# Inverting the 64x64 triangles of two head pairs side by side, every second period

## The chip, the cores and the metric

The kernel runs on one core of one Trainium2 chip. The metric is the device time of one execution in microseconds (us). The core has five engines with a queue each: TensorE (PE, matmuls; PEld are its weight loads), VectorE (DVE), ScalarE (ACT), GpSimd (POOL) and SyncE (SP), which here issues the DMAs.

## The reference

Two layers over 256 tokens of width 2048. Layer 0 is RWKV-7 time mixing and an MLP, layer 1 chunked attention and an MLP; every sub-layer is normalised and modulated by shift, scale and gate vectors that are products of a vector `c` with a large matrix `w_ada`. The change lies in the time mixing, whose core is a recurrence for each of 32 heads of 64:

```python
def step(S, inp):
    r_t, w_t, k_t, v_t, kk_t, a_t = inp
    sa = jnp.einsum('bhvk,bhk->bhv', S, -kk_t)
    S = (S * w_t[:, :, None, :] + sa[..., None] * (kk_t * a_t)[:, :, None, :]
         + v_t[..., None] * k_t[:, :, None, :])
    y = jnp.einsum('bhvk,bhk->bhv', S, r_t)
    return S, y
mod = c @ w_ada[layer] + b_ada[layer]
```

## The kernel before

The recurrence is done in four chunks of 64 tokens. Within a chunk it is a triangular system, and the kernel inverts its 64x64 unit triangle for every head and chunk. Two heads make a pair (128 partitions); there are 16 pairs. A pair goes through four stages:

- `proj_steps` (dense work): the k and r projections, 16 weight blocks each, every block a 128x512 and a 128x256 matmul (L401, L402). Weights come as raw float32 tiles of 512 KB (`raw`), are rounded to a high half `wH` on ACT (L367), and DVE makes the low half `wL` (L370).
- `early`: decay, keys and norms, mostly on DVE and ACT.
- `invert`: the Gram matrices (L100, tile `gr`), then five levels of doubling. A level has two calls of `tiles`, each 16 matmuls of 32x32 on four 32x32 blocks of the array (L106, tile `iv`; the last level 8): first `al` (masked by POOL, L233) times `tt` (DVE's transpose of `u`, L229), copied by ACT to `xs` (L235), then `xs` times `u`, added to `u` by DVE (L246). `uf` holds the finished inverse.
- `late`: the chain over the four chunks, 16 short steps of PE, ACT and DVE (tiles `chn`, `py`, `zs`).

The loop of `layer_a` over `p` runs periods; in each one four neighbouring pairs are in the four stages, so there are 16 + 3 periods. A period has 16 slots. In a slot the small stages (`late`, `invert`, `early`) each take their share of steps and the dense stage takes its own; `tc.issue_after` makes them alternate on PE. In the last three periods no projection is left, and `out_steps` (part of the output projection `w_o`, 44 steps of six matmuls) is the dense work; `DRAIN_STEPS` says how many of its steps each of them gets. In six slots of every period (`ADA_SLOTS`) one tile of the modulation is done: a DMA of 512 KB into `raw` and one multiply-add of 128x1024 on DVE (L443, tile `acc`). Weights and modulation tiles share one ring of `RAW_BUFS` = 6 raw buffers, and all their DMAs go in order through the SP queue, as do the small tables `lw` (L121) and `lg` (L123).

Engines run their queues in order. [...]

Of the kernel before, what the change touches and what calls it, by code (L numbers as in the profile page):

```python
# [12 lines left out]
F32 = mybir.dt.float32  # L13
F32R = mybir.dt.float32r
AF = mybir.ActivationFunctionType
ALU = mybir.AluOpType
# [60 lines left out]
class Pair:  # L77
# [24 lines left out]
    def tiles(self, o, lhsT, rhs, pairs):  # L102

        for c in range(4):
            for R, K in pairs:
                self.b.nc.tensor.matmul(o[QS[K], c, :], lhsT[QS[R], c, :], rhs[QS[R], c, :], start=True, stop=True,  # L106
                                        tile_position=(H * R, H * K))

# [8 lines left out]
    def early(self):  # L117
        b, nc, j, k, r, v, s, ch = self.b, self.b.nc, self.j, self.k, self.r, self.v, self.s, self.ch
        pw, vec, cst, e01 = b.pw, b.vec, b.cst, self.e01
        lw = pw.tile([96, 2, P], F32, tag="lw", bufs=2, name="lw")  # L120
        nc.sync.dma_start(out=lw, in_=b.d["lora2"][j, :96, 0:2])  # L121
        self.lg = pw.tile([P, 2, P], F32, tag="lg", bufs=2, name="lg")
        nc.sync.dma_start(out=self.lg, in_=b.d["lora2"][j, :, 2:4])  # L123
# [24 lines left out]
        self.pc = pw.tile([P, 4, 1], F32, tag="pc", bufs=3, name="pc")  # L148
# [9 lines left out]
        self.bh, self.kh = s("bh", 2), s("kh", 2)  # L158
# [8 lines left out]
        kr = self.kr = self.big("kr", 3)  # L167
# [9 lines left out]
        bk = self.bk = pw.tile([P, 3, 4, C], F32, tag="bk", bufs=3, name="bk")  # L177
# [9 lines left out]
    def invert(self):  # L187
        b, nc, s, ch, kr, bk, bh, kh = self.b, self.b.nc, self.s, self.ch, self.kr, self.bk, self.bh, self.kh
        cst, pp = b.cst, b.pp

        def every(name):
            return cst(name).unsqueeze(1).to_broadcast([P, 4, H])

        def half(name, bufs):
            return b.pw.tile([P, 4, H], F32, tag=name, bufs=bufs, name=name)


        ui = cst("ui").unsqueeze(1).to_broadcast([P, 4, P])
        ts = []
        for src in (bh, kh):  # L200
            t = s()
            nc.gpsimd.tensor_tensor(out=ch(t), in0=ch(src), in1=self.pc.to_broadcast([P, 4, C]), op=ALU.mult)
            ts.append(t)
        pg = pp.tile([P, 4, P], F32, tag="gr", bufs=1, name="gr")
        self.each(lambda c: pg[:, c, :], lambda c: ch(bh)[:, c, :], lambda c: kr[:, c, :])
        ar = self.ar = s("ar", 2)
        nc.vector.tensor_tensor(out=ch(ar), in0=pg[:, :, C:P], in1=ui[:, :, C:P], op=ALU.mult)


        da, co, u = half("da", 2), half("co", 2), half("u", 2)  # L210
        for i, K in enumerate(QS):
            n = H * (i % 2)
            nc.scalar.copy(da[K], pg[K, :, n:n + H])
            if i % 2 == 0:
                nc.scalar.mul(co[K], pg[K, :, H:C], -1.0)
        nc.gpsimd.tensor_tensor(out=u, in0=da, in1=every("lev0"), op=ALU.mult)
        yield
        nc.vector.tensor_tensor(out=u, in0=u, in1=every("eye_h"), op=ALU.add)

        pt = b.psm().rearrange("p (a c k) -> p a c k", a=2, c=4)  # L220
        for i, t in enumerate(ts):
            self.each(lambda c: pt[:, i, c, :], lambda c: ch(t)[:, c, :], lambda c: cst("eye"))
        nc.scalar.copy(bk[:, 0:2], pt)
        yield
        uf = self.u = b.uf[self.j % 2]
        down, up = ((0, 1), (2, 3)), ((1, 0), (3, 2))
        for l in range(1, 6):
            tt_, xs = half("tt", 1), half("xs", 1)
            nc.vector.transpose(out=tt_.rearrange("p c t -> p (c t)"), in_=u.rearrange("p c t -> p (c t)"))  # L229
# [12 lines left out]
            yield
            pi = pp.tile([P, 16, H], F32, tag="iv", bufs=1, name="iv")[:, 0:4, :]
            if l < 5:
                self.tiles(pi, xs, u, [(i, i) for i in range(4)])
                nc.vector.tensor_tensor(out=u, in0=u, in1=pi, op=ALU.add)  # L246
            else:
                self.tiles(pi, xs, u, up)
                for K in QS[::2]:
                    nc.vector.tensor_copy(uf[K, :, H:C], pi[K])  # L250
            if l == 2:
                pg = pp.tile([P, 4, P], F32, tag="gr", bufs=1, name="gr")
                self.each(lambda c: pg[:, c, :], lambda c: ch(kh)[:, c, :], lambda c: kr[:, c, :])
                mk = self.mk = self.big("mk", 2)
                nc.vector.tensor_tensor(out=mk, in0=pg, in1=ui, op=ALU.mult)
            yield

    def late(self):
# [7 lines left out]
        for c in range(4):  # L266
            pch = pp.tile([P, 3, C], F32, tag="chn", bufs=1, name="chn")
# [38 lines left out]
        rg = s("sl", 3)  # L306
# [4 lines left out]
        for i in range(2):  # L311
            nc.tensor.matmul(pg, self.lg[:, i, :], self.tg[:, i, :], start=(i == 0), stop=(i == 1))
# [5 lines left out]
class Body:  # L318
    RAW_BUFS = 6
    W_BUFS = 3  # L320
    DRAIN_STEPS = (14, 14, 16)
    ADA_SLOTS = (1, 3, 6, 9, 11, 14)

# [15 lines left out]

    @contextmanager  # L340
# [8 lines left out]
    def raw(self, src, shape=None, ada=False):  # L349
# [3 lines left out]
        else:  # L353
            t = self.wp.tile([P, HK * P], F32, tag="raw", bufs=self.RAW_BUFS, name="raw")
# [18 lines left out]
    def weight_part(self, src, lo, hi):  # L373

        half, at = lo // HK * HK * P, lo % HK * P
        t = self.wp.tile([P, HK * P], F32, tag="raw", bufs=self.RAW_BUFS, name="raw")
# [185 lines left out]
    def run(self):  # L562
# [16 lines left out]
        self.lazy, self.fins, self.ada_pool = False, iter(()), None  # L579
        self.ada_done = set()  # L580
# [4 lines left out]
        with ExitStack() as st:  # L585
# [7 lines left out]
            nxt = self.out_proj(self.pp, "w_o", self.y_hl, (0, 2), "g_mlp0", (0, 4), (0, 3), self.o_ps)  # L593
            sp.close()
            with ExitStack() as s2:
                pp = s2.enter_context(tc.tile_pool(name="ps_m0", bufs=2, space=bass.MemoryType.PSUM, reuse_waits="tile"))
                self.psm = lambda: pp.tile([P, 512], F32, tag="m", bufs=2, name="m")
                s2.enter_context(self.ada_room(5))
                nxt = self.mlp(s2, pp, 0, *nxt, "g_kv", ("kv", 1), ("kv", 0))
            with ExitStack() as s2:  # L600
                pp = s2.enter_context(tc.tile_pool(name="ps_at", bufs=2, space=bass.MemoryType.PSUM, reuse_waits="tile"))
                self.psm = lambda: pp.tile([P, 512], F32, tag="m", bufs=1, name="m")
                s2.enter_context(self.ada_room(3))
# [15 lines left out]
    def layer_a(self, st, sp):  # L619
# [6 lines left out]
        with ExitStack() as s1:  # L626
# [5 lines left out]
            pb = self.np = s3.enter_context(tc.tile_pool(name="pb", bufs=1))  # L632
            h = ph.tile([P, KT, T + 1], F32, name="h")
# [154 lines left out]
            for i in range(4):  # L788
                v_part(3, i, "tm"[i % 2])
            s3.close()  # L790
# [13 lines left out]
        with ExitStack() as s1:  # L804
# [5 lines left out]
            self.uf = [pw.tile([P, 4, C], F32, name=f"uf_{i}") for i in range(2)]  # L810
# [6 lines left out]
            def proj_steps(pr):  # L817
                for dst, hl in (("k", xk), ("r", xr)):
# [14 lines left out]
            def out_steps():  # L833
# [3 lines left out]
                sums, todo = self.o_ps, [(n, 0, HK) for n in range(4)] + [(n, HK, KT - 2) for n in range(4)]  # L837
                for n, lo, hi in todo + [(n, 0, HK) for n in range(4, 8)]:
# [349 lines left out]
```

## Time and profile before

| | |
|---|---|
| time, median of 3 runs | 2720.82 us (2719.59 to 2724.55) |
| profiled execution: time, span | 2718.15 us, 2716.3 us |
| PE, DVE, ACT, POOL busy | 97%, 77%, 50%, 9% of the span |
| granted TensorE clock, mean | 0.993 |
| time mixing with its periods | from 210 us to 753 us of the span |

In the tables of windows each engine has its busy time and the number of instructions in the window, then come the granted TensorE clock, the busy share of the DMA engines and their rate. A row of the timeline has the start, the time it is in flight, and xN for N instructions merged; one small float32 matmul is two records there. Matmuls overlap, so what a group costs PE is read from its start to the start of the next group.

### The profile page before, as it was taken

To read this page: it belongs to the slowest core of one execution; us is meant where nothing else is said; L and a number is where in the kernel's file an instruction comes from. 1 tells how busy PE (TensorE), PEld (TensorE's weight loads), DVE (VectorE), ACT (ScalarE), POOL (GpSimd) and SP (SyncE) were. 2 spreads that over 40 slices of the span, in tenths; PEclk is the share of its full clock that TensorE was granted. 3 is DMA by queue.
4 is the path that set the end of the run, shared out by engine and by line. 5 is a ranking of instruction groups with operands and counts; after the bars stand their busy time and mean duration, and the time that the engine had idled before them with its cause. 6 is when DMAs were issued, how large, how long until landed. Compare 5 with 4: busy or idle time off the path is not lost.

```text
span 2716.3 us, 58473 instructions
## 1 busy us (share of the span) xinstructions
PE 2646.6 (97%) x23690; PEld 2237.0 (82%) x23690; DVE 2098.3 (77%) x3109; ACT 1347.4 (50%) x2432; POOL 235.0 (9%) x368
## 2 busy tenths in 40 slices
PE   6998999999999999999999999999999999999997
PEld 3777777777889888888888898877898888888886
DVE  5779887778788798888988898899987556555555
ACT  3344554455455536445355554465565364453553
POOL 0002232232210000000000100000100000000002
PEclk8999999999999999999999999999999999999999
DMA  9967665555587799888988768887857555555553
GB/s 334 314 232 254 201 194 172 161 175 172 190 279 256 251 342 332 309 310 317 331 318 319 249 225 309 310 292 252 285 194 258 186 189 189 187 186 187 187 188 122
DMA packets 217390, 662.64 MB, mean 244 GB/s; under 512 B 21408, under 2 KB 68896, under 8 KB 217120
## 3 DMA queue, kind: packets, MB, share of 16 engines
q1 hardware_dynamic: 215056, 656.36, 71.3%
q8 instruction: 186, 3.05, 0.4%
q10 hardware_dynamic: 2064, 2.54, 0.3%
q14 instruction: 84, 0.69, 0.1%
HBM read 656.72 MB, written 2.10 MB: 243 GB/s over the span
## 4 chain that ended last, share of the span: by engine, by line
PE 86%; DVE 4%; DMA 2%; issue 2%; ACT 1%; POOL 0%; DVEq 0%; SPq 0%; ACTq 0%; POOLq 0%
PE pj L401 45%; PE pj L402 22%; PE iv L106 2%; PE pj L391 2%; PE pj L392 2%; PE pj L390 2%; PE gr L100 1%; DVE wL L370 1%; DVE acc L443 1%; PE ms L100 1%; PE o L390 1%; PE ms L110 1%; PE chn L270 1%; DMA rada<-w_ada 1%; PE chn L277 1%
## 5 line engine op out<-in xcount | busy, mean ns | idle before, releaser
L370 DVE TENSOR_TENSOR wL<-raw,wH 128x1024 fp32r<-128x1024 f32 x772 | 941.7, 1221 | 372.1 <-ACT wH L367 367.5
L401 PE MATMUL pj<-aHL,wH 128*128 128x512 f32 x3328 | 1214.8, 405 | 2.6 <-DVE v L748 1.4
L367 ACT CAST wH<-raw 128x1024 fp32r<-128x1024 f32 x772 | 805.7, 1045 | 812.0 <-PE pj L401 654.4
L402 PE MATMUL pj<-aHL,wL 128*128 128x256 f32 x3328 | 939.3, 282 | 2.6 <-DVE e L812 1.7
L401 PEld LDWEIGHTS pj<-aHL,wH 128*128 128x128 f32 x3328 | 628.4, 189 | 155.4 <-issue 10.5
L401 PE MATMUL pj<-hHL,wH 128*128 128x512 f32 x2048 | 724.6, 399 | 0.0
L402 PEld LDWEIGHTS pj<-aHL,wL 128*128 128x128 f32 x3328 | 628.5, 189 | 7.7 <-DVE wL L370 2.2
L402 PE MATMUL pj<-hHL,wL 128*128 128x256 f32 x2048 | 574.6, 281 | 0.0
L401 PEld LDWEIGHTS pj<-hHL,wH 128*128 128x128 f32 x2048 | 384.8, 188 | 96.0 <-DVE hHL L954 0.2
L402 PEld LDWEIGHTS pj<-hHL,wL 128*128 128x128 f32 x2048 | 386.8, 189 | 0.1
L443 DVE SCALAR_TENSOR_TENSOR acc<-rada,ct,acc 128x1024 f32<-128x1024 f32 x254 | 324.9, 1279 | 7.4 <-DMA rada<-w_ada 7.0
L507 POOL TENSOR_TENSOR ss<-ss,sq 128x256 f32<-128x256 f32 x56 | 55.2, 986 | 1591.0 <-ACT sq L506 1590.7
L979 DVE SCALAR_TENSOR_TENSOR x<-pj,mod,x 128x256 f32<-128x256 f32 x256 | 123.3, 482 | 58.0 <-PE pj L402 54.4
L443 DVE SCALAR_TENSOR_TENSOR acc<-raw,ct,acc 128x1024 f32<-128x1024 f32 x106 | 139.4, 1315 | 6.3 <-DMA raw<-w_ada 6.2
L951 ACT ACTIVATE t<-t 128x256 f32<-128x256 f32 x112 | 46.8, 418 | 128.2 <-DVE t L923 128.2
L392 PE MATMUL pj<-aHL,wL 128*128 128x258 f32 x384 | 108.5, 283 | 1.5 <-DVE wL L370 1.5
L391 PE MATMUL pj<-aHL,wH 128*128 128x258 f32 x384 | 109.6, 286 | 0.0
L390 PE MATMUL pj<-aHL,wH 128*128 128x258 f32 x384 | 109.6, 285 | 0.0
L392 PEld LDWEIGHTS pj<-aHL,wL 128*128 128x128 f32 x384 | 73.9, 193 | 1.8 <-DVE wL L370 1.7
L391 PEld LDWEIGHTS pj<-aHL,wH 128*128 128x128 f32 x384 | 73.4, 191 | 0.1
L390 PEld LDWEIGHTS pj<-aHL,wH 128*128 128x128 f32 x384 | 72.9, 190 | 0.2
L953 ACT ACTIVATE t<-t 128x256 f32<-128x256 f32 x128 | 53.4, 417 | 3.5
(244 smaller groups left out, 2851.3 us busy)
## 6 DMA issues: line engine op xcount, KB each, us to landing
raw<-w_up SPq DMA_DIRECT2D x256, 512.0 KB, 3.9
raw<-w_down SPq DMA_DIRECT2D x256, 512.0 KB, 4.1
rada<-w_ada SPq DMA_DIRECT2D x206, 512.0 KB, 5.6
raw<-w_ada SPq DMA_DIRECT2D x114, 512.0 KB, 4.4
rawa<-w_ada SPq DMA_DIRECT2D x64, 512.0 KB, 6.9
rada<-w_ada_kv SPq DMA_DIRECT2D x64, 512.0 KB, 5.8
raw<-w_k SPq DMA_DIRECT2D x32, 512.0 KB, 4.9
raw<-w_r SPq DMA_DIRECT2D x32, 512.0 KB, 4.6
```

The costliest lines, as they stand in the source:

```text
L100: self.b.nc.tensor.matmul(o(c)[K], lhsT(c)[K], rhs(c)[K], start=True, stop=True)
L106: self.b.nc.tensor.matmul(o[QS[K], c, :], lhsT[QS[R], c, :], rhs[QS[R], c, :], start=True, stop=True, tile_position=(H * R, H * K))
L367: nc.scalar.copy(Hf, raw)
L370: eng.tensor_tensor(out=Lf, in0=raw, in1=Hf, op=ALU.subtract)
L390: nc.tensor.matmul(ps, H[:, i, :], a(kt)[:, 0, :], start=(first and kt == 0), stop=False)
L391: nc.tensor.matmul(ps, H[:, i, :], a(kt)[:, 1, :], start=False, stop=False)
L392: ins = nc.tensor.matmul(ps, L[:, i, :], a(kt)[:, 0, :], start=False, stop=(last and kt == KT - 1))
L401: nc.tensor.matmul(ps, H[:, i, :], a(kt), start=(kt == 0), stop=False)
L402: ins = nc.tensor.matmul(ps[:, 0, :], L[:, i, :], a(kt)[:, 0, :], start=False, stop=(kt == KT - 1))
L443: nc.vector.scalar_tensor_tensor(out=self.acc, in0=raw, scalar=ck, in1=self.acc, op0=ALU.mult, op1=ALU.add)
L507: (eng or nc.gpsimd).tensor_tensor(out=self.ss, in0=self.ss, in1=sq, op=ALU.add)
L979: nc.vector.scalar_tensor_tensor(out=x, in0=ps[:, i, :], scalar=self.mods[(layer, 5)][:, n:n + 1], in1=x, op0=ALU.mult, op1=ALU.add)
```

## The change

`invert` takes a list of pairs and works on tiles of 8 instead of 4 chunks, so one call of `tiles` has 32 small matmuls, and one DVE, ACT or POOL instruction covers two pairs. It runs in periods 3, 5, ..., 17 only. A pair therefore waits up to one period longer: `LAG` is 4, there are 20 periods, and several tiles have one buffer more (`kr`, `bk`, `bh`, `kh`, `pc`, `ar`, `mk`). The drain has four periods with 10, 6, 14 and 14 of the 44 `out_steps`; the second halves of `w_o` move to their end. No modulation tiles are taken in periods 0 and 1; periods 2 to 9 take one more, in slot 7. The mixing takes 116 of the 360 modulation tiles instead of 114. To make room the ring of raw buffers is 4 in the mixing, with 2 more outside it (`more_raw`); `lg` has one buffer and is loaded in the second chunk of `late`, `lw` is loaded at the start of the projection.

```diff
-    def invert(self):
+    @staticmethod
+    def invert(pairs):
+        N = 4 * len(pairs)
...
+        def tiles(o, lhsT, rhs, ks):
+            for c in range(N):
+                for R, K in ks:
+                    nc.tensor.matmul(o[QS[K], c, :], lhsT[QS[R], c, :], rhs[QS[R], c, :], start=True, stop=True,
+                                     tile_position=(H * R, H * K))
...
+        for i, pr in enumerate(pairs):
+            own = slice(4 * i, 4 * i + 4)
...
+            pg = pp.tile([P, 4, P], F32, tag="gr", bufs=1, name="gr")
+            pr.grams(pg, pr.bh)
...
+            yield
...
         for l in range(1, 6):
-            tt_, xs = half("tt", 1), half("xs", 1)
+            tt_, xs = half("tt"), half("xs")
...
+            if 2 <= l < 2 + len(pairs):
+                pr = pairs[l - 2]
                 pg = pp.tile([P, 4, P], F32, tag="gr", bufs=1, name="gr")
...
     def late(self):
         for c in range(4):
+            if c == 1:
+                lg = pw.tile([P, 2, P], F32, tag="lg", bufs=1, name="lg")
+                nc.sync.dma_start(out=lg, in_=b.d["lora2"][j, :, 2:4])
...
-    RAW_BUFS = 6
-    DRAIN_STEPS = (14, 14, 16)
+    RAW_BUFS = 4
+    DRAIN_STEPS = (10, 6, 14, 14)
+    ADA_MORE = 8
...
-                sums, todo = self.o_ps, [(n, 0, HK) for n in range(4)] + [(n, HK, KT - 2) for n in range(4)]
-                for n, lo, hi in todo + [(n, 0, HK) for n in range(4, 8)]:
+                sums = self.o_ps
+                for n, lo, hi in [(n, 0, HK) for n in range(8)] + [(n, HK, KT - 2) for n in range(4)]:
...
-            for p in range(NPAIR + 3):
+            for p in range(NPAIR + LAG):
...
+                if p >= LAG:
+                    live.append([pairs[p - LAG].late(), 16, 0])
+                if p % 2 and 3 <= p < NPAIR + 2:
+                    live.append([Pair.invert(pairs[p - 3:p - 1]), 14, 0])
+                if 0 < p <= NPAIR:
+                    live.append([pairs[p - 1].early(), Pair.EARLY, 0])
...
-                    if slot in self.ADA_SLOTS:
+                    if p >= 2 and (slot in self.ADA_SLOTS or slot == 7 and p < 2 + self.ADA_MORE):
                         self.ada()
```

The order of PE in the middle of the mixing, before: `iv` are the inverse's calls, `chn` and `py` steps of `late`, `pj` the projection.

```order
L106 MATMUL iv<-tt,al 32x32 x16
L270 MATMUL chn<-bk,mk 64x64 x2
L273 MATMUL chn<-zs,kr 64x64 x2
L401 MATMUL pj<-aHL,wH 128x512
L106 MATMUL iv<-u,xs 32x32 x16
L402 MATMUL pj<-aHL,wL 128x256
L277 MATMUL chn<-g,uf_2235 64x64 x2
L280 MATMUL py<-mk,bk 64x64 x2
L283 MATMUL py<-kr,zs 64x64 x2
L401 MATMUL pj<-aHL,wH 128x512
L402 MATMUL pj<-aHL,wL 128x256
```

After, in a period with an inverse:

```order
L295 MATMUL chn<-zs,kr 64x64 x2
L440 MATMUL pj<-aHL,wH 128x512
L206 MATMUL iv<-tt,al 32x32 x32
L441 MATMUL pj<-aHL,wL 128x256
L440 MATMUL pj<-aHL,wH 128x512
L441 MATMUL pj<-aHL,wL 128x256
L299 MATMUL chn<-g,uf_2235 64x64 x2
```

The calls are twice as long, and every second period has none: from the projection's first to the end of the last `py<-tg,lg`, PE's list has 161 rows `iv` before and 80 after, and the shape of the matmul (full array, 64-row or 32-row tiles) changes 703 times before and 597 times after. A float32 full-array call of `early` or `late` (`ms` or `py`, 128x256) is followed by a smaller shape 31 times before and 12 times after; the transposed `v` (`ms<-csts,v`) stands in 34 pieces before and 17 after.

The order of DVE in periods 0 and 1, before: `acc` are modulation tiles, `k` and `r` end a projection.

```order
L829 TENSOR_TENSOR k<-pj,k 128x256
L370 TENSOR_TENSOR wL<-raw,wH 128x1024
L443 SCALAR_TENSOR_TENSOR acc<-raw,ct,acc 128x1024
L370 TENSOR_TENSOR wL<-raw,wH 128x1024
L443 SCALAR_TENSOR_TENSOR acc<-raw,ct,acc 128x1024
L130 TENSOR_SCALAR s<-ms,vecs 128x256
L443 SCALAR_TENSOR_TENSOR acc<-raw,ct,acc 128x1024
L829 TENSOR_TENSOR r<-pj,r 128x256
L130 TENSOR_SCALAR s<-ms,vecs 128x256
L370 TENSOR_TENSOR wL<-raw,wH 128x1024
```

After:

```order
L877 TENSOR_TENSOR k<-pj,k 128x256
L409 TENSOR_TENSOR wL<-raw,wH 128x1024 x2
L120 TENSOR_SCALAR s<-ms,vecs 128x256
L877 TENSOR_TENSOR r<-pj,r 128x256
L120 TENSOR_SCALAR s<-ms,vecs 128x256
L409 TENSOR_TENSOR wL<-raw,wH 128x1024
```

The twelve `acc` of these two periods are gone from between the weights.

The order of the SP queue around the load of `lg`, before: `w_k` and `w_r` are weights, `w_ada` modulation tiles.

```order
L357 DMA raw<-w_k 128x1024 x2
L123 DMA lg<-lora 128x256
L357 DMA raw<-w_ada 128x1024
L121 DMA lw<-lora 96x256
L357 DMA raw<-w_ada 128x1024 x2
L357 DMA raw<-w_r 128x1024 x2
```

After:

```order
L396 DMA raw<-w_k 128x1024
L288 DMA lg<-lora 128x256
L396 DMA raw<-w_k 128x1024
L865 DMA lw<-lora 96x256
L396 DMA raw<-w_ada 128x1024 x3
L396 DMA raw<-w_r 128x1024 x2
```

In some periods the second half of the next `w_k` now stands behind `lg`, which with one buffer waits for the end of the previous pair's `late` (L312).

More of the change, by code (lines that the diff above doesn't have):

```diff
@@ L119, in early @@
         pw, vec, cst, e01 = b.pw, b.vec, b.cst, self.e01
[L120 to L123, printed above, removed]
+        lw = self.lw
         z = b.psm()
@@ L198, in invert @@
         ui = cst("ui").unsqueeze(1).to_broadcast([P, 4, P])
+        da, co, u = half("da"), half("co"), half("u")
         ts = []
[L200 to L215, printed above, removed]
+        for i, pr in enumerate(pairs):
+            own = slice(4 * i, 4 * i + 4)
+            tp = []
+            for src in (pr.bh, pr.kh):
+                t = pr.s()
+                nc.gpsimd.tensor_tensor(out=pr.ch(t), in0=pr.ch(src), in1=pr.pc.to_broadcast([P, 4, C]), op=ALU.mult)
+                tp.append(t)
+            ts.append(tp)
+            pg = pp.tile([P, 4, P], F32, tag="gr", bufs=1, name="gr")
+            pr.grams(pg, pr.bh)
+            pr.ar = pr.s("ar", 3)
+            nc.vector.tensor_tensor(out=pr.ch(pr.ar), in0=pg[:, :, C:P], in1=ui[:, :, C:P], op=ALU.mult)
+            for q, K in enumerate(QS):
+                n = H * (q % 2)
+                nc.scalar.copy(da[K, own], pg[K, :, n:n + H])
+                if q % 2 == 0:
+                    nc.scalar.mul(co[K, own], pg[K, :, H:C], -1.0)
+            yield
@@ L216, in invert @@
         nc.gpsimd.tensor_tensor(out=u, in0=da, in1=every("lev0"), op=ALU.mult)
+        pairs[0].transposed_keys(ts[0])
         yield
         nc.vector.tensor_tensor(out=u, in0=u, in1=every("eye_h"), op=ALU.add)
[L220 to L223, printed above, removed]
+        if len(pairs) > 1:
+            pairs[1].transposed_keys(ts[1])
@@ L311, in late @@
         for i in range(2):
-            nc.tensor.matmul(pg, self.lg[:, i, :], self.tg[:, i, :], start=(i == 0), stop=(i == 1))
+            nc.tensor.matmul(pg, lg[:, i, :], self.tg[:, i, :], start=(i == 0), stop=(i == 1))
         nc.vector.scalar_tensor_tensor(out=rg, in0=v, scalar=b.vec("ln_b", j), in1=rg, op0=ALU.add, op1=ALU.add)
@@ L353, in raw @@
         else:
-            t = self.wp.tile([P, HK * P], F32, tag="raw", bufs=self.RAW_BUFS, name="raw")
+            t = self.raw_tile()
         if shape is not None:
@@ L375, in weight_part @@
         half, at = lo // HK * HK * P, lo % HK * P
[L376 removed]
+        t = self.raw_tile()
         n = at if hi == KT else 0
@@ L809, in layer_a @@
             e01 = [pw.tile([P, 4, C + 1], F32, name=f"e01_{i}") for i in range(2)]
-            self.uf = [pw.tile([P, 4, C], F32, name=f"uf_{i}") for i in range(2)]
+            self.uf = [pw.tile([P, 8, C], F32, name=f"uf_{i}") for i in range(2)]
             for e, u in zip(e01, self.uf):
```

97 lines of the change are left out of this document (61 added, 36 removed).

## The prediction

> **What bounds the kernel now.** I read the page first, then the windows by stretch of the mixing, then the waits of PE there, and last PE's timeline, since the waits alone don't tell what a busy PE is busy with.
>
> ```profile
> span 2716.3 us, 58473 instructions
> PE 2646.6 (97%) x23690; PEld 2237.0 (82%) x23690; DVE 2098.3 (77%) x3109; ACT 1347.4 (50%) x2432; POOL 235.0 (9%) x368
> ```
>
> PE is in use nearly all the time, so what counts is PE's work and the few places where it stops. The stretches shown are, in order: period 0, period 1, period 2, periods 4 to 15, the first two drain periods, the last one.
>
> ```profile
> 210.42:225.69 15.27, 13.62 (x75) 11.66 (x76) 14.88 (x28) 9.22 (x22) 0.56 (x2) 1.00 0.75 248
> 225.69:244.70 19.01, 15.79 (x97) 12.86 (x96) 18.53 (x26) 9.52 (x20) 6.50 (x5) 0.86 0.90 329
> 244.70:272.71 28.01, 24.56 (x514) 19.07 (x510) 23.89 (x42) 12.93 (x35) 8.53 (x14) 0.97 0.66 210
> ...
> 303.25:675.87 372.62, 368.91 (x6954) 281.76 (x6950) 295.76 (x566) 190.50 (x530) 113.26 (x168) 1.00 0.56 176
> 675.87:731.60 55.73, 55.41 (x1192) 46.55 (x1182) 48.05 (x82) 25.90 (x72) 15.27 (x23) 1.00 0.67 218
> 731.60:753.00 21.40, 21.40 (x280) 18.63 (x280) 7.92 (x15) 6.01 (x16) 0.00 (x0) 1.00 0.23 67
> ```
>
> Periods 4 to 15 take 372.62 / 12 = 31.05 us each and PE idles 3.7 us in all twelve; the drain idles 0.3 us. The first three periods idle 1.65 + 3.22 + 3.45 = 8.3 us, with DVE at 97% in two of them, and the clock is below 1 there (0.86 and 0.97). The longest wait of PE in periods 4 to 15, and two of periods 0 to 2:
>
> ```profile
> PE iv L106 <- DVE zs L292: 2.8, 3, 1.4
> ```
>
> ```profile
> PE gr L100 <- DVE bh L169: 3.2, 1, 3.2
> ...
> PE pj L401 <- DVE v L748: 1.4, 1, 1.4
> ```
>
> So in steady state nothing is waited for: PE's own list is the bound. What a piece of that list costs is seen in the timeline (start, time in flight):
>
> ```profile
> 447.49 0.28 PE L283 MATMUL py<-kr,zs 64*64 64x64 f32 x4
> 447.61 0.28 PE L100 MATMUL ms<-csts,v 64*64 64x64 f32 x2
> 447.81 0.45 PE L106 MATMUL iv<-tt,al 32*32 32x32 f32 x32
> 448.20 0.51 PE L401 MATMUL pj<-aHL,wH 128*128 128x512 f32 x1
> 448.54 0.28 PE L402 MATMUL pj<-aHL,wL 128*128 128x256 f32 x1
> 448.66 0.40 PE L401 MATMUL pj<-aHL,wH 128*128 128x512 f32 x1
> 448.89 0.28 PE L402 MATMUL pj<-aHL,wL 128*128 128x256 f32 x1
> 449.10 0.33 PE L298 MATMUL py<-ar,sa 64*64 64x64 f32 x4
> ...
> 452.05 0.59 PE L110 MATMUL py<-sq,csts 128*128 128x256 f32 x2
> 452.29 0.59 PE L401 MATMUL pj<-aHL,wH 128*128 128x512 f32 x1
> 452.71 0.28 PE L402 MATMUL pj<-aHL,wL 128*128 128x256 f32 x1
> ...
> 453.19 0.59 PE L110 MATMUL ms<-rkp,csts 128*128 128x256 f32 x2
> 453.71 0.33 PE L270 MATMUL chn<-bk,mk 64*64 64x64 f32 x4
> ```
>
> Start to start, a dense pair costs 0.23 + 0.12 us (448.66, 448.89, and the 0.12 from 448.54 to 448.66). The first L401 after a smaller shape takes 0.34 (448.20 to 448.54), and the L402 ahead of a smaller shape 0.21 (448.89 to 449.10): leaving and re-entering the full array costs 0.09 + 0.11 = 0.20 us. A call of `tiles` costs 0.39 (447.81 to 448.20). A full-array float32 call costs 0.24 ahead of dense work (452.05 to 452.29) but 0.52 ahead of a smaller shape (453.19 to 453.71).
>
> **The change part by part.** All sums are against the profiled execution, 2718.15 us; the median of the runs is 2.67 us higher, which I add at the end.
>
> (a) Inverse calls. 160 calls (161 rows, one split) become 80 of twice the matmuls. Of the 0.45 us in flight of 32 records one record alone is about 0.19 (the mean of this row, below), so 31 further starts take 0.26 us, 8 ns each; the other 0.13 of the 0.39 is the change of shape. A doubled call should cost 0.39 + 32 x 0.008 = 0.65 instead of 0.78: 80 x 0.13 = 10 us less. Bounds: nothing (it costs twice), and 80 x 0.39 / 2 = 16 us, if half of the second call hides. I take -10, since the 8 ns are from the same instruction.
>
> ```profile
> L106 PE MATMUL iv<-tt,al 32*32 32x32 f32 x2048 | 29.2, 194 | 5.8 <-DVE zs L292 2.8 <-DVE tt L229 2.8
> L229 DVE STREAM_TRANSPOSE tt<-u 128x128 f32<-128x128 f32 x80 | 24.2, 303 | 0.5
> L246 DVE TENSOR_TENSOR u<-u,iv 128x128 f32<-128x128 f32 x64 | 18.1, 282 | 16.7 <-PE iv L106 16.3
> L443 DVE SCALAR_TENSOR_TENSOR acc<-raw,ct,acc 128x1024 f32<-128x1024 f32 x106 | 139.4, 1315 | 6.3 <-DMA raw<-w_ada 6.2
> ```
>
> [...]
>
> (b) What stands between the calls. In the new list the shape changes 106 times less; some 80 of these changes belong to calls of (a). The rest by kind: 19 float32 full-array calls fewer stand ahead of a smaller shape (31 to 12). Each saves 0.28, of which about 0.08 comes back, as a dense L401 behind such a call costs 0.42 (452.29 to 452.71) rather than 0.34: 19 x 0.2 = 3.8 us. The transposed `v` is cut into 17 pieces less, at about one change of shape of 0.1 to 0.17 each: 2 to 3 us. Dense work is interrupted some 10 times less, at 0.20: 2 us. Together -8 us; bounds 0 (other changes fill the places) and -12.
>
> The other calls (Gram matrices, transposed keys, `late`, `early`, projections) are the same in number. The halves on ACT, DVE and POOL cost nothing on PE as long as they are in time; see (e).
>
> (c) The first periods. Before, periods 0 to 2 lose 8.3 us of idling and, by the clock, 0.14 x 19.01 + 0.03 x 28.01 = 3.5 us at half speed, worth about 2.7: 11 us. The lost clock lies right behind the idling (windows of 5 us), and the chain that ended last runs through DVE there, over modulation tiles:
>
> ```profile
> 235.00:240.00 5.00, 2.16 (x13) 1.61 (x11) 5.00 (x10) 1.10 (x4) 1.79 (x1) 0.94 1.03 411
> 240.00:245.00 5.00, 4.62 (x22) 3.58 (x22) 4.22 (x6) 1.25 (x2) 2.61 (x2) 0.50 0.71 239
> ```
>
> ```profile
> 237.73 1.20 DVE acc L443
> 238.92 0.40 DVE s L164
> ```
>
> Twelve tiles of 1.3 us leave DVE here (15.8 us), more than all that is lost. But period 2 now has no inverse, so PE has only some 15 us to do in it (like period 1, whose PE is busy 15.79), while DVE still has the weights (4 x 1.2), seven tiles (9.2) and what else period 1 shows on it (18.53 - 6 x 1.3 - 4 x 1.2 = 5.9), 20 us: PE waits some 5 us there, or DVE carries it into period 3. Of the `v L748` wait, the end of the phase before, most stays. I take -4; bounds 0 (the stop only moves) and -9.
>
> (d) The drain. The same 44 dense steps lie in 64 slots instead of 48: 20 slots have none, before 4. Where a slot has none, the short chain shows:
>
> ```profile
> 720.39 0.28 PE L283 MATMUL py<-kr,zs 64*64 64x64 f32 x4
> 720.76 0.33 PE L287 MATMUL chn<-bk 64*64 64x64 f32 x4
> ```
>
> L283 needs 0.12 (like the pieces above), so PE stood still for 0.25 us until `sa` was there. With an inverse in the slot a step must wait for DVE (0.28 + 0.30, doubled width more) and may cost 0.9. 16 further slots x 0.3 = +5 us; bounds 0 and +14. The extra period has no work of its own.
>
> (e) Steady waits. Before, other work stood between two calls of a level (in the order shown, two `chn` groups and an L401), which covered ACT's copy; in some places of the new list it is one projection matmul. The copy is now twice as wide, and so are DVE's two operations. An inverse's DVE work is 5 x 0.30 + 4 x 0.28 and about 2 us of masks and copies (an estimate from their widths), 4.6 us per pair. So periods alternate: one with two inverses, PE 31 + 7 - 1 = 36 to 37 us; one with none, about 24 us (a pair's inverse is ten calls of 0.39 and three groups of Gram matrices and transposes of about 1 us, as this one, together 7 us):
>
> ```profile
> 460.78 1.10 PE L100 MATMUL ms<-csts,s 64*64 64x64 f32 x32
> ```
>
> DVE has 295.76 / 12 = 24.6 per period before; without an inverse, and with the seventh tile, 24.6 - 4.6 + 1.3 = 21.3 of 24, with two about 29 of 36. Nothing is over its limit, but in the short periods DVE runs at nearly 90%, and an `acc` or `wL` of 1.2 to 1.3 us in front of a `zs` is no longer hidden by a slot of 1.94 us, but must fit one of 1.5. I take +5 us over the mixing, about 0.4 per period; bounds 0 and +20 (the rival of the raw ring).
>
> Later phases: two modulation tiles less, 2.6 us on DVE, which PE doesn't wait for there; the ring has six buffers again. Nothing.
>
> Sum: -10 - 8 - 4 + 5 + 5 = -12: 2706.1 on the profiled execution, 2708.8 on the median; I say 2708.
>
> **The rivals.** First, the cover holds: (d) and (e) cost together 2 us, (c) gives its 9. Then it is -25, 2696. For it speaks that PE waited for nothing in twelve periods although ACT and DVE were busy half and four fifths; against it the 20 bare slots.
>
> Second, it doesn't do what it says: doubled calls cost twice, and the drain's 14 us are paid. -8 - 4 + 14 + 2 = +4, no difference that can be told, 2722 to 2725. Against it stand the 8 ns.
>
> Third, it gets slower by the ring of four raw buffers. The DMA queue waits for buffers already with six, and a load takes over 4 us to land, to which the two halves' rounding comes:
>
> ```profile
> SPq L357 <- DVE acc L443: 62.1, 33, 5.9
> ```
>
> ```profile
> raw<-w_ada SPq DMA_DIRECT2D x72, 512.0 KB, 4.2
> raw<-w_k SPq DMA_DIRECT2D x20, 512.0 KB, 5.1
> ```
>
> ```profile
> L370 DVE TENSOR_TENSOR wL<-raw,wH 128x1024 fp32r<-128x1024 f32 x772 | 941.7, 1221 | 372.1 <-ACT wH L367 367.5
> ...
> L367 ACT CAST wH<-raw 128x1024 fp32r<-128x1024 f32 x772 | 805.7, 1045 | 812.0 <-PE pj L401 654.4
> ```
>
> The ring is full before, so ten tiles in 31.05 us and six buffers mean 18.6 us per tile from issue to release. With four buffers and eleven tiles in a short period of 24 us it is 8.7 us, of which 4.2 to 5.1 are the landing. A second half of `w_k` that is issued only when `lg` is free, at the end of the period, takes 5.1 to land, 1.05 on ACT (L367's mean) and 1.2 on DVE, 7.4 us, and PE needs it after half a projection, a quarter of a period, 6 us in a short one. That is 1.4 us in each of six short periods, 8 us, and eats less than what is won. It decides from 3.7 us per short period on (22 / 6), when the tiles stop DVE as well; at 5 us it is +30 - 22 + 5 = +13, 2734.
>
> **How the numbers follow.** A measurement here tells 0.2% from no change, 5.4 us. The forecast, -6 to -22 us, gets 0.57; the first rival (2687 to 2699) 0.2; the second 0.11; the third 0.12. Faster is the sum of the first two, 0.77; same 0.11; slower 0.12. The bounds of the parts add up to -37 and +34; the range leaves out the ends of the first and third cases: 2689 to 2727. The likeliest case's own range is 2699 to 2715.
>
> **What would show it.** (a) The timeline after shows a call of 64 records with its next start 0.65 us later, and L106 has half the groups. (b) PE's list from the first projection to the last L312 takes about 18 us less, the odd periods 35 to 38 us and the even ones 22 to 25. (c) No `acc` before period 2, no clock of 0.5 at 240 us, but PE waiting for DVE in period 2. (d) Waits of `iv` and `chn` in the four drain periods of some 5 us. (e) In periods 4 to 15 PE idles 5 to 10 us rather than 3.7. It is wrong if the 32x32 records don't run at 8 ns when they are 64, if `wL` of a `w_k` shows up as what PE waits for in the even periods, or if `DVE acc <- DMA` grows from the 6 us that it has.

## The result: slower by 25 us

The changed kernel takes 2745.49 us in the median (five runs, 2740.91 to 2747.03) and the kernel before 2720.82 (2715.76 to 2724.55): the ratio is 1.0088, 95% interval 1.0073 to 1.0102. The forecast was 2708. The profiled execution of the changed kernel took 2740.91 us, its span is 2739.0 us, 22.7 us more than the 2716.3 of before, and where these 22.7 us come from can be read from the two traces.

The head of the page after, with the row of PE's own instruction queue (packets, MB, share of the DMA engines):

```profile
span 2739.0 us, 58162 instructions
PE 2646.1 (97%) x23690; PEld 2244.6 (82%) x23690; DVE 2089.8 (76%) x3013; ACT 1342.9 (49%) x2384; POOL 195.4 (7%) x296
q8 instruction: 186, 3.05, 0.4%
```

PE has as many records (entries of the trace: one matmul or one weight load each) and as much busy time as before. The windows by stretch (period 0, 1, 2, 3, a long period, a short one, periods 4 to 15 together, the four drain periods together, the drain's second and third period, and one dip of the clock):

```profile
209.00:222.36 13.36, 12.49 (x70) 10.86 (x70) 11.14 (x25) 10.56 (x23) 0.99 (x2) 1.00 0.51 156
222.36:236.09 13.73, 13.73 (x89) 11.82 (x88) 11.70 (x21) 9.33 (x20) 2.25 (x3) 1.00 0.64 211
236.09:255.99 19.90, 17.42 (x110) 14.36 (x110) 19.16 (x26) 9.86 (x21) 7.42 (x7) 0.93 0.84 270
255.99:294.02 38.03, 33.05 (x803) 25.31 (x801) 32.42 (x51) 20.28 (x53) 11.96 (x17) 0.95 0.66 208
444.09:486.01 41.92, 38.38 (x905) 30.13 (x901) 31.83 (x52) 18.29 (x51) 9.71 (x12) 0.96 0.58 183
486.01:507.53 21.52, 21.52 (x202) 16.30 (x202) 16.96 (x29) 12.56 (x30) 6.29 (x7) 1.00 0.59 186
294.02:673.93 379.91, 363.72 (x6986) 281.92 (x6986) 299.09 (x496) 182.15 (x480) 83.38 (x110) 0.99 0.58 184
673.93:769.70 95.77, 88.90 (x1590) 75.23 (x1591) 60.36 (x97) 34.07 (x92) 10.05 (x16) 0.93 0.54 170
...
698.00:722.00 24.00, 20.49 (x605) 17.08 (x602) 19.21 (x26) 7.94 (x23) 3.31 (x5) 0.86 0.76 236
722.00:751.00 29.00, 26.80 (x467) 22.73 (x466) 14.01 (x20) 8.63 (x20) 2.52 (x4) 0.88 0.48 151
...
475.00:478.50 3.50, 3.50 (x93) 2.88 (x84) 0.99 (x1) 1.42 (x2) 0.00 (x0) 0.51 0.51 154
```

Four stretches make up the difference. To the end of period 3 the changed kernel is 9.2 us ahead (294.02 against 303.25). Periods 4 to 15 take 379.9 us against 372.6, +7.3. The drain takes 95.8 us against 77.1, +18.6. After the mixing come another 6 us. The sum is +22.7. One piece of it only moves: with the longer lag a `late` leaves periods 0 to 3 and comes into the drain. A short period has a projection, an `early` and a `late` in 22.3 us (the mean of the six), period 1 the first two in 13.73, so a `late` is 8.6 us. Without it the start is level with before (-0.6) and the drain 10 us worse.

The short periods are as forecast (21.5 to 23.8 us, PE never idle). The long ones are not: 39.1 to 43.3 us, and PE, which idled 3.7 us in all twelve periods before, now idles 16.2. The waits of PE in periods 4 to 15 (us in total, times, longest):

```profile
PE iv L206 <- issue: 8.0, 8, 2.6
PE iv L206 <- DVE tt L247: 3.9, 7, 1.0
PE gr L100 <- issue: 1.5, 1, 1.5
PE ms L100 <- issue: 1.2, 1, 1.2
```

Most of it is "issue": PE waits for nothing that the profile shows. Before there were two such waits in these periods, of 0.6 and 0.2 us. PE's timeline shows one, in a call that breaks off in the middle:

```profile
456.63 0.75 PE L206 MATMUL iv<-u,xs 32*32 32x32 f32 x64
457.31 0.50 PE L440 MATMUL pj<-aHL,wH 128*128 128x512 f32 x1
...
463.18 0.59 PE L206 MATMUL iv<-u,xs 32*32 32x32 f32 x44
465.10 0.38 PE L206 MATMUL iv<-u,xs 32*32 32x32 f32 x20 [1.33 <-issue]
465.41 0.98 PE L100 MATMUL gr<-kr,kh 64*64 64x128 f32 x14
```

The first call runs through: 0.68 us from its start to the next, as forecast (0.65). The second issues 44 of its 64 records, halts for 1.33 us, and goes on. Each operand of this call is written by one operation that is over before the first record starts at 463.18 us (`u` on DVE at 460.02, `xs` on ACT at 462.06), so no work of DVE or ACT is what the other 20 wait for.

What the halts have in common stands in the trace's records of the queue q8. Its 186 packets of 16384 bytes bring 3.05 MB, and PE has 47599 records to share them: 23690 matmuls, 23690 loads and 219 of its sequencer, nearly all semaphores. That is 64.0 bytes each and 255.9 records to a packet (256.1 before, with 47634), so I count a packet as 256 of PE's instructions. If all these records, those of the sequencer too, are counted from the first, all 13 halts of the mixing fall on the same place of a block: between record 449 + 256k and the next, for whole numbers k. (11 of them stand in PE's waits as "issue"; two are shorter, 0.34 and 0.38 us from one start to the next.) And each ends 2.2 to 2.7 us after the start of a q8 packet, 1.2 to 1.5 us after its end. My reading of this is that PE had used up its instructions, and the next block was not there yet; the trace shows the place and the times, not the cause. The kernel before has one halt at such a place, of 0.6 us, 2.3 us after the start of a packet. The block before a halt was used up in 1.9 to 4.5 us. From period 4 to the end of the mixing, 19 of 67 blocks are used up within 4.5 us, before 4 of 66. The rows above say why: the long period has 905 + 901 records, 1152 of them in its ten doubled calls (the two of the last level are half as long), and where two such calls stand with only pieces of a `late` and of a Gram group between them, 256 of them go by in 1.9 us; the short period has 404 in 21.5 us.

Four of the halts cost twice: behind four of the seven over 1 us the granted clock is 0.5 for 3.41 us (the last row of the windows above is the dip that follows the halt ending at 474.67). In this dip an L440 and an L441 take 0.43 and 0.21 us to the next start, behind it 0.24 and 0.12, and a call of 64 records takes 1.01 us after 0.68. My estimate, from the clock of 0.5, is that a dip costs half of its length, 1.7 us. Before, there was none in periods 4 to 15.

The last 6 us are lost far behind the mixing, at the end of the first MLP: one wait, and the clock behind it.

```profile
PE pj L429 <- DVE ks L593: 4.2, 1, 4.2
```

```profile
1585.00:1590.00 5.00, 1.15 (x5) 1.18 (x6) 5.00 (x11) 1.66 (x3) 0.00 (x0) 0.78 1.00 344
1590.00:1595.00 5.00, 5.00 (x27) 5.00 (x26) 4.40 (x10) 2.13 (x4) 0.00 (x0) 0.53 0.97 343
```

Four modulation tiles stand in DVE's order ahead of the row sums there (1576.7 to 1586.2 us), while PE waits for the first operand of the attention. Before, PE was busy throughout (40.0 of the 40 us from 1560 on).

### The profile page after: what moved, and what is told of

It is laid out like the page before. It is cut to its first block, busy times and chain, and to the rows that moved or that the text cites. A ratio compares the mean times of both kernels' runs of the same rounds, so it can differ in the third digit from the quotient of the medians.

```text
span 2739.0 us, 58162 instructions
## 1 busy us (share of the span) xinstructions
PE 2646.1 (97%) x23690; PEld 2244.6 (82%) x23690; DVE 2089.8 (76%) x3013; ACT 1342.9 (49%) x2384; POOL 195.4 (7%) x296
## 3 DMA queue, kind: packets, MB, share of 16 engines
q8 instruction: 186, 3.05, 0.4%
## 4 chain that ended last, share of the span: by engine, by line
PE 80%; DVE 5%; DMA 4%; issue 3%; ACT 2%; POOL 0%; SPq 0%; DVEq 0%; ACTq 0%; POOLq 0%
PE pj L440 43%; PE pj L441 22%; DMA rada<-w_ada 2%; PE iv L206 2%; DVE wL L409 1%; DVE acc L482 1%; PE pj L430 1%; PE pj L429 1%; PE pj L431 1%; DMA raw<-w_ada 1%; PE gr L100 1%; PE o L429 1%; PE chn L299 1%; PE py L334 1%; PE ms L100 0%
## 5 line engine op out<-in xcount | busy, mean ns | idle before, releaser
L440 PE MATMUL pj<-aHL,wH 128*128 128x512 f32 x3328 | 1217.6, 406 | 2.0 <-DVE x L960 1.1
L441 PE MATMUL pj<-aHL,wL 128*128 128x256 f32 x3328 | 940.2, 283 | 1.1 <-DVE wL L409 1.1
L440 PEld LDWEIGHTS pj<-aHL,wH 128*128 128x128 f32 x3328 | 629.5, 189 | 156.1 <-issue 11.9
L440 PE MATMUL pj<-hHL,wH 128*128 128x512 f32 x2048 | 721.6, 397 | 0.0
L441 PEld LDWEIGHTS pj<-aHL,wL 128*128 128x128 f32 x3328 | 629.8, 189 | 6.4 <-DVE wL L409 1.7
L441 PE MATMUL pj<-hHL,wL 128*128 128x256 f32 x2048 | 574.0, 281 | 0.0
L440 PEld LDWEIGHTS pj<-hHL,wH 128*128 128x128 f32 x2048 | 384.4, 188 | 93.6 <-DVE hHL L1006 0.2
L441 PEld LDWEIGHTS pj<-hHL,wL 128*128 128x128 f32 x2048 | 386.8, 189 | 0.1
L482 DVE SCALAR_TENSOR_TENSOR acc<-raw,ct,acc 128x1024 f32<-128x1024 f32 x108 | 143.7, 1331 | 12.8 <-DMA raw<-w_ada 12.3
```

What stands on the lines that cost most here:

```text
L440: nc.tensor.matmul(ps, H[:, i, :], a(kt), start=(kt == 0), stop=False)
L441: ins = nc.tensor.matmul(ps[:, 0, :], L[:, i, :], a(kt)[:, 0, :], start=False, stop=(kt == KT - 1))
L482: nc.vector.scalar_tensor_tensor(out=self.acc, in0=raw, scalar=ck, in1=self.acc, op0=ALU.mult, op1=ALU.add)
```

## The experiments

**Late tiles alone.** The first periods without the rest of the change:

```diff
-                    if slot in self.ADA_SLOTS:
+                    if p >= 2 and (slot in self.ADA_SLOTS or slot == 7 and p < 14):
```

> The kernel before, with one thing of the change alone: no modulation tile in periods 0 and 1; the twelve tiles come one each in the eighth slot of periods 2 to 13, so that there are 114 as before. Theory A (my term c, -4 us, bounds 0 and -9): PE's 8 us of idling in periods 0 to 2 and the half clock at 240 us go in part, 2717 us (2712 to 2721). Theory B (the stop only moves, or DVE is full in later periods by the seventh tile): no difference, 2719 to 2723, and the idling stands in periods 1 and 2 as before.

2707.65 us in the median against 2715.7 for the kernel before beside it: ratio 0.9963 (0.995 to 0.9975), so it is faster by 8 to 10 us. Windows of period 1, period 2 and periods 4 to 15:

```profile
223.10:236.80 13.70, 13.70 (x99) 11.58 (x98) 12.65 (x22) 9.31 (x20) 3.95 (x5) 1.00 0.73 242
236.80:268.60 31.80, 29.68 (x492) 23.00 (x491) 26.96 (x47) 14.55 (x43) 13.51 (x17) 0.89 0.65 212
295.00:667.80 372.80, 371.73 (x7033) 283.64 (x7031) 307.45 (x579) 191.05 (x528) 112.94 (x168) 1.00 0.60 190
```

Period 1 takes 13.7 us and not 19.0, and by the end of period 3 the kernel is 8.3 us ahead (295.0 against 303.25); the periods after it take what they took before. Theory A, and by the difference near the far end of its bounds (-9); the time itself lies below its range, since the kernel before was faster here too.

**Each call twice.** Doubled calls in the kernel before, with nothing else of the change:

```diff
-        for c in range(4):
+        for c in 2 * list(range(4)):
```

> The kernel before, but every call of 16 inverse matmuls is issued twice in a row (the second one writes the same values), so that PE sees calls of 64 records as in the changed kernel while all operations on ACT, DVE and POOL stay as narrow as before and the periods stay alike. The plain price is 160 x 0.26 us = 42 us, 2762 us. Theory S (PE runs out of instructions: it halts at the end of a block of 256 records when these took less than some 4 us): halts of 0.3 to 2.8 us without a semaphore in the middle of calls, each at the same place of a block of 256 records, 10 to 20 of them, with half-clock windows behind the longer ones; 2775 to 2800 us. Theory D (the longer chain of wide copies and transposes on ACT and DVE is what costs): no such halts beyond the one or two of the kernel before, 2758 to 2766 us.

2813.23 us (one run), 97.5 more than before. The calls that run through take 0.68 us to the next start after 0.38 (those of the last level 0.62 after 0.37), so the plain price is 46 us and not 42, and 51 are something else. In the mixing there are 29 halts, all behind record 449 + 256k, 34 us from start to start, and the granted clock is 0.5 for 34 us in place of 7, by half some 14 us. PE has 56854 records now, 256 for each packet of its queue again. The queue, PE's waits in periods 2 to 15, and the longest halt in the timeline:

```profile
q8 instruction: 222, 3.64, 0.5%
```

```profile
PE iv L106 <- issue: 15.1, 17, 2.7
```

```profile
479.58 0.59 PE L106 MATMUL iv<-tt,al 32*32 32x32 f32 x45
482.88 0.53 PE L106 MATMUL iv<-tt,al 32*32 32x32 f32 x19 [2.71 <-issue]
483.33 0.80 PE L401 MATMUL pj<-aHL,wH 128*128 128x512 f32 x1
```

ACT and DVE work here just as before (in periods 4 to 15 190.7 and 293.4 us, before 190.5 and 295.8), so wide operations aren't what makes the halts. Theory S, which had put the price too low (2800 at most).

**The two pairs as steps of their own.** Same periods, calls of 32 records again (shown: one of the two halves of a level):

```diff
+            for o in halves:
-                tiles(pi, al, tt_, [(q, q) for q in range(4)])
-                nc.scalar.copy(xs, pi)
+                tiles(pi, al, tt_, [(q, q) for q in range(4)], o)
+                nc.scalar.copy(xs[:, o], pi[:, o])
+                yield
...
-                    live.append([Pair.invert(pairs[p - 3:p - 1]), 14, 0])
+                    live.append([Pair.invert(pairs[p - 3:p - 1]), 24, 0])
```

The steps of a slot are taken in turn, one of each part, so that others stand between the two halves.

> The changed kernel, but within each level the two pairs are issued as steps of their own with other steps between: calls of 32 records again, and ACT, DVE and POOL work on each pair apart, in the same periods (two inverses in the odd ones, none in the even ones). The price of 80 more calls is 80 x 0.13 = 10 us, other shape changes some 4. Theory S (a block of 256 records in too short a time, whatever the length of a call): a slot of a long period still holds as many records, spread over one tenth more time, so most of the 13 halts stay (7 or more): 2745 to 2757 us. Theory S64 (it is the unbroken run of 64 records that starves PE): no halts, -20 + 14, 2735 to 2742 us. Theory D (wide operations): the waits for tt and xs go, the halts aren't touched.

2758.67 us (2747.67, the profiled execution, to 2760.87), ratio 1.0144 (1.0124 to 1.0163). PE's waits in periods 3 to 15, and a long period:

```profile
PE iv L206 <- DVE u L266: 3.1, 3, 2.3
PE iv L206 <- issue: 2.3, 3, 1.0
PE iv L206 <- DVE tt L250: 1.7, 3, 0.9
```

```profile
384.10:424.60 40.50, 40.41 (x915) 30.62 (x912) 32.74 (x63) 18.92 (x57) 13.40 (x20) 1.00 0.60 191
```

No theory had it right. 4 halts of 13 are left, although 17 of 67 blocks are still used up within 4.5 us: none of these is faster than 3.2 us, while the changed kernel has five at 1.9 to 3.3 us, of which four end in a halt. So in these two kernels it goes by how fast a block is used up, the fastest ones are made by unbroken runs of 64, and my limit of some 4 us was too coarse. (One of the 4 halts follows a block of 5.7 us that itself began with a halt.) The wait for `tt` is small, that for `u` new. But the long period takes 40.5 us with PE busy in 40.4 of them, and periods 4 to 15 take 384.9 us, 5 more than in the changed kernel: the splitting costs more than the halts did. I put that down to changes of shape: there are 556 of them in these periods here and 459 in the changed kernel, which at some 0.1 us each, an estimate from the 0.09 and 0.11 us read in the timeline of before, is 10 us. No run separates it.

**Half the records.** The same tiles, read as bfloat16 (the inverse keeps 8 bits):

```diff
+            lhsT, rhs = (t.bitcast(mybir.dt.bfloat16)[:, :, 1::2] for t in (lhsT, rhs))
```

> The changed kernel, but the inverse's matmuls read the upper halves of the same tiles as bfloat16, so that each is one record with one load and not two (the inverse keeps 8 bits; everything else, every operation on ACT, DVE and POOL too, is as in the changed kernel). Calls have 32 records. Theory S: 320 of some 905 records of a long period are gone, so hardly a block of 256 is used up within 4 us: 0 to 3 halts, no half-clock windows behind them, and the list is 80 x 0.26 = 21 us shorter; 2700 to 2712 us. Theory D (the chain over ACT and DVE bounds the long periods): PE waits for xs and tt instead, the long periods shrink by less than 1 us each, 2735 us or more.

2708.92 us (2705.68 to 2717.09), ratio 0.9974 (0.9959 to 0.9989). One halt of 0.6 us in the mixing, and a granted clock of 1.00 over periods 4 to 15. PE has 42970 records, and its queue brings fewer packets to match. (288 matmul records of a long period are gone and not 320, since the last level's calls are half as long.) The queue, PE's waits in periods 4 to 15, and their window:

```profile
q8 instruction: 168, 2.75, 0.4%
```

```profile
PE iv L207 <- DVE tt L248: 5.5, 9, 0.9
...
PE pj L441 <- issue: 0.5, 1, 0.5
```

```profile
295.30:642.40 347.10, 338.79 (x5267) 256.89 (x5266) 294.72 (x495) 182.33 (x480) 89.79 (x113) 1.00 0.63 198
```

The call is shorter than I had reckoned:

```profile
397.96 0.37 PE L207 MATMUL iv<-tt,al 32*32 32x32 bf16 x32
398.26 0.65 PE L100 MATMUL gr<-kr,kh 64*64 64x128 f32 x8
```

0.30 us and not 0.68 - 0.26, so the 48 full calls of these periods give 0.38 us each and the 12 of the last level 0.33, together 22 us. The rest of the 32.8 (379.9 - 347.1) is halts and clock, 15.8 in the changed kernel, less 2 to 3 us of new waits on DVE; that would be some 2 us more than came.

**The control.** The same, each call twice:

> The kernel with the inverse's matmuls in bfloat16 of 8 bits, with each call issued twice (the second one writes the same values): 64 records to a call again, as in the changed kernel, with the operands of the run with half the records. A control for that run. Theory S (the number of records in a short time): halts at the same place of a block of 256 records are back, 8 to 18 of them; 2735 to 2755 us. If it was something else in the operands (type, stride) that took the halts away: at most 3 halts, and only the plain price of 80 x 0.26 = 21 us, 2725 to 2732 us.

```diff
-            for c in range(N):
+            for c in 2 * list(range(N)):
```

2759.57 us (one run, above theory S's range), 14 halts, again all behind record 449 + 256k. A call that halts (timeline):

```profile
412.09 0.40 PE L207 MATMUL iv<-u,xs 32*32 32x32 bf16 x34
415.57 0.36 PE L207 MATMUL iv<-u,xs 32*32 32x32 bf16 x30 [3.08 <-issue]
```

So it was the number of records that took the halts away, not the type.

**114 tiles.**

```diff
-    ADA_MORE = 8
+    ADA_MORE = 6
```

> The changed kernel with six instead of eight seventh modulation tiles, so that the time mixing takes 114 as before and not 116. Theory T (the two tiles more let the modulation run out of step with the weights of the later phases: four accumulations stand on DVE in front of the row sums at the end of the first MLP, PE waits 4.2 us for ks there and runs at half clock for 6.8 us): that wait and that clock are gone, 5 to 7 us faster than the changed kernel, 2738 to 2741 us. Theory U (it is a consequence of the mixing's other order or of its end 17 us later): the wait stays, 2744 to 2747 us.

2734.77 us (2731.9 to 2744.1), ratio 1.0073 (1.0051 to 1.0096). By the medians 10.7 us less than the changed kernel, by the ratios, whose intervals overlap, some 4 us: the times alone don't settle it. The trace does: PE waits for nothing from 1560 to 1600 us, and the place of the 4.2 us is full.

```profile
1580.00:1585.00 5.00, 5.00 (x44) 5.00 (x43) 4.93 (x10) 3.16 (x5) 0.69 (x6) 1.00 0.78 284
1585.00:1590.00 5.00, 5.00 (x44) 5.00 (x43) 5.00 (x13) 3.30 (x5) 0.00 (x0) 1.00 0.39 132
```

The wait and the clock of 0.53 are gone; the run with the two pairs as steps of their own and the one with half the records, both with 116 tiles, have the wait of 4.2 us at this place too. Theory T, though the median lies below its range.

**Another order of the output steps.**

```diff
-    DRAIN_STEPS = (10, 6, 14, 14)
+    DRAIN_STEPS = (4, 12, 14, 14)
```

> The changed kernel with the 44 output steps in the four drain periods as 4, 12, 14, 14 and not 10, 6, 14, 14. Theory I (the drain loses where the last inverse has no dense work beside it: 3.5 us of idling and a clock of 0.86 in its period): the drain shrinks by 3 to 6 us from 95.8 us, and no half clock follows in that period. Theory B (each bare slot costs the same, wherever it is; their number stays 20): the drain stays at 95 to 97 us.

2739.85 us (one run). The drain's second period, its last two, and the whole drain:

```profile
698.40:722.40 24.00, 21.25 (x656) 17.01 (x653) 18.87 (x28) 5.68 (x14) 1.75 (x4) 0.86 0.68 216
722.40:764.80 42.40, 42.40 (x544) 36.30 (x542) 20.61 (x31) 13.67 (x32) 2.36 (x4) 1.00 0.48 147
674.40:764.80 90.40, 86.68 (x1590) 72.69 (x1589) 60.86 (x96) 34.32 (x93) 12.34 (x16) 0.96 0.58 183
```

The drain is 5.4 us shorter with as many bare slots. But the idling in its second period is 2.8 us after 3.5 and the clock there is still 0.86: the gain lies behind it, where PE doesn't pause any more and has its full clock (before this edit 2.2 us of idling and a clock of 0.88). So theory I has the size right and the place wrong. Of the 5.4 us the span keeps only 1.0 (2738.0 against 2739.0): what comes behind the mixing takes 3.9 us longer here, and one run doesn't tell why.

**The ring alone.** The kernel before with the change's four raw buffers and its places for the `lw` and `lg` loads:

```diff
-    RAW_BUFS = 6
+    RAW_BUFS = 4
...
-        self.lg = pw.tile([P, 2, P], F32, tag="lg", bufs=2, name="lg")
-        nc.sync.dma_start(out=self.lg, in_=b.d["lora2"][j, :, 2:4])
...
+            if c == 1:
+                lg = pw.tile([P, 2, P], F32, tag="lg", bufs=1, name="lg")
+                nc.sync.dma_start(out=lg, in_=b.d["lora2"][j, :, 2:4])
```

> The kernel before with the change's buffers alone: four raw buffers in the time mixing and six elsewhere, and the loads of lw and lg at the places that the change gives them. Rival 3 of the prediction (the ring slows the loads, and PE waits for wL of w_k behind the lg load): periods of 31 us leave more room than the short ones of the changed kernel, so 0.5 to 1.4 us per period, 2726 to 2740 us, with PE waiting for wL. If the ring costs nothing: 2716 to 2723 us, no wait of PE for wL, though DVE's wait for the modulation tiles may double from 6 us.

2721.63 us (2713.28 to 2727.07), ratio 1.0005 (0.999 to 1.0019): no difference. PE's waits for weights in the mixing:

```profile
PE pj L417 <- ACT wH L383: 3.5, 2, 2.0
...
PE pj L418 <- DVE wL L386: 1.6, 2, 0.8
```

There are such waits, 5.1 us in all, which the kernel before doesn't have, but they don't add up to a loss that can be measured. DVE's wait for the modulation tiles is 6.9 us after 5.7, so it doesn't double here. Two halts behind record 449 + 256k, of 1.3 and 0.4 us, show that they aren't the changed kernel's alone.

**What is left of both.** Late tiles and half the records, each pair by itself; and the changed kernel with half the records, 114 tiles and the other output steps:

> The kernel before (every pair's inverse by itself) with no modulation tiles in periods 0 and 1, and with the inverse's matmuls reading the upper halves of their tiles as bfloat16: 16 records to a call and not 32, the inverse keeps 8 bits. Theory S and the list as the bound: 160 calls x 16 records x 8 ns = 20 us less than the run with late tiles alone, 2684 to 2692 us. Theory D (with less of its own work PE waits for the chain over ACT and DVE): half of it is lost in waits for tt and xs, 2694 to 2704 us.

> The changed kernel with the three things that the runs found mended: the inverse's matmuls read upper halves as bfloat16 (8 bits, half the records), 114 modulation tiles, and output steps 4, 12, 14, 14. If the costs add up: 2709 - 6 - 5 = 2698 us (2692 to 2704). Against the run with late tiles, half the records and every pair by itself (2679 us) it says what the inverses side by side are worth once no halt is left: periods 4 to 15 should take 8 us less than its 354.7 us, and the drain some 15 us more than its 73 us, since a `late` of 8 us has moved into it and the last inverse stands there with little dense work; so it stays slower by 10 to 20 us. If the halts were all that made the change slow, it would be faster than that run: 2665 to 2675 us.

2678.52 us for the first (ratio 0.9854, 0.9839 to 0.9869), 2691.4 for the second (0.9895, 0.9878 to 0.9911). Both lie below the ranges that I had given. Periods 4 to 15 of the first, and one of its calls with what follows; of the second period 3, periods 4 to 15 and the drain:

```profile
289.00:643.70 354.70, 354.51 (x5319) 263.62 (x5318) 309.15 (x582) 190.44 (x531) 121.26 (x168) 1.00 0.64 203
```

```profile
399.83 0.27 PE L107 MATMUL iv<-u,xs 32*32 32x32 bf16 x16
400.03 0.50 PE L402 MATMUL pj<-aHL,wH 128*128 128x512 f32 x1
```

```profile
257.80:294.70 36.90, 27.06 (x477) 21.40 (x478) 32.03 (x51) 18.89 (x54) 10.96 (x16) 0.88 0.62 203
294.70:639.40 344.70, 338.19 (x5262) 256.62 (x5262) 293.59 (x494) 182.05 (x477) 93.39 (x111) 1.00 0.62 197
639.40:726.30 86.90, 81.64 (x1303) 68.40 (x1302) 62.50 (x97) 34.43 (x94) 12.55 (x16) 0.98 0.61 197
```

Without halts the inverses side by side win 10.0 us in periods 4 to 15 (344.7 against 354.7). The drain, with one `late` more, takes 13.6 us more than the 73.3 of the first. Period 3 has PE idle for 9.8 us beside a busy DVE, and periods 4 to 15 begin 5.7 us later (294.7 against 289.0). Another 4 us are lost behind the mixing, for which no run gives the cause. So pairing doesn't pay here, even mended; half the records and late tiles do. With the inverse in full float32, the kernel before with late tiles (2707.65) is the fastest of all that ran.

## Why the prediction was wrong

It forecast -12 us on the profiled execution and +22.7 came, a miss of 35 us.

(a) The price of the doubled call was near: 0.68 us and not 0.65. But a single call takes 0.38 in the mean, so a doubled one saves 0.08 and not 0.13 (0.12 in the last level), 7 us in all and not 10. What failed is the step from this price to the sum: that PE, given a list, issues it at that price. I looked for waits on engines, buffers and transfers; PE's own instruction supply was not among the terms, though the page of the profile names its queue (186 packets, 3.05 MB) and the rows of before give the rate (32 records and 32 loads in 0.39 us). Nor was it among the bounds: "it costs twice" was meant as the price of the records. In its place the runs show 13 halts at the ends of blocks of 256 instructions, and the clock behind them.

(a), (b) and (e) in periods 4 to 15: three quarters of -10 - 8 + 5 are -9.8 us, and +7.3 came. The halts there are 10.7 us of idling and three dips of the clock 5.1; without these 15.8 us it would be -8.5, near the forecast. That is taken away by reckoning, and two runs stand behind it: with half the records one halt is left, and the mended pairing wins 10.0 us in these periods. (There a doubled call saves 2 x 0.20 - 0.30 = 0.10 us, about what it does in float32, and 60 of them 6 us; the other 4 would be (b), which no run tests by itself.) The waits for `tt` that (e) priced came in about that size: 3.9 us.

(c) The rule alone (no modulation tiles in periods 0 and 1) is worth 8.3 us by the end of period 3, not 4: I took half of what its bound allowed. (The 3.5 us "at half speed" are what the clock costs by half; it stood at 0.5 for 6.8 us.) In the changed kernel nearly all of it is lost again at once (level with before, once the moved `late` is taken out). The wait for DVE in period 2 came with half of the 5 us that the working names (2.5 us, DVE busy for 19.16 of 19.90), but period 3 then idles 5.0 us, of which 1.6 are a halt, and with half the records 8.6 without a halt, 7.7 of it waiting for `tt`: there DVE's chain holds the first double inverse. "DVE carries it into period 3" stood in the working, without a price.

(d) The drain cost 10 us beside the moved `late`, with a forecast of 5 and a bound of 14; in the one run with the other order of the dense steps 5 of them are gone. "The extra period has no work of its own" is true, but the `late` of 8.6 us that it moves out of the early periods belonged in (c) and (d), with opposite signs.

"Later phases: nothing" was wrong: with two tiles fewer left to do, four of them come to stand at another place, where PE waits for DVE. That is 6 us.

Of the rivals the third named the right sign by a mechanism that isn't there: the ring of four costs nothing in the kernel before, and in the changed one DVE's wait for its tiles doubles, from 5.7 to 12.3 us, without PE waiting for weights in the mixing. In us, the miss is 17 in periods 4 to 15, 12 in the start and the drain together (+9.4 came; -4 + 5 and a quarter of (a), (b) and (e), -3, were forecast) and 6 behind them. What of the 12 is halts, waits for DVE and clock was not separated.

## What to carry to other kernels

Where small matmuls are packed more densely, count instructions, not only their time: of the blocks of 256, loads included, that went by here in less than 4 us, 65 of 108 ended in a halt, of the slower ones 27 of 786. The halts showed as idle time without a releaser in the middle of a call or group. That all 13 gaps fell on one place of a block of 256 records is what pointed to PE's supply; fewer records (one pass and not two) left one halt of 0.6 us, where another order left 4 and cost more than it saved (384.9 us in periods 4 to 15 after 379.9). And the change of lag moved a `late` of 8.6 us from the start to the end of the pipeline: take such a piece out of both before reading either.

## What the runs showed of the hardware

The packets of PE's instruction queue have 16384 bytes, one for every 256 of its records: 255.9 in the changed kernel, 256.1 before and with doubled calls, 255.8 with half the records. In the changed kernel PE goes on from a halt 2.2 to 2.7 us after a packet starts, and all 13 halts, 29 with doubled calls and 14 in the control fall behind record 449 + 256k. In the mixing of the twelve kernels profiled here, 24 of 32 blocks that are used up in under 3 us end in a halt, 41 of 76 at 3 to 4 us, 20 of 153 at 4 to 5, 7 of 263 at 5 to 7, and none of 370 above.

In the changed kernel the clock fell to 0.5 for 3.41 us behind halts of 1.05 to 2.58 us, but not behind others of 1.25 to 1.48 us; what tells them apart was not settled.

A bfloat16 call of 32 records takes 0.30 us to the next start, a float32 call of 32 records 0.38 (before); for 64 records it is 0.58 (the control) and 0.68. So in these calls a record in bfloat16 is cheaper in itself, not only rarer.
